# Scan coefficients and products in a PSUM bank per direction, input tables one block ahead, the last kernel block behind the first scan steps

## The chip, the cores and the metric

One core of one Trainium2 chip runs the whole forward pass of a small encoder trunk for one sequence of 512 positions and 1024 channels, in float32. The metric is the device time of one execution in microseconds. Five engines work side by side, each through its own queue in order: PE (matrix products), DVE and POOL (elementwise), ACT (elementwise with functions, and copies), SP (starts most DMA transfers). They wait for each other through semaphores. A line such as L669 is a line of the kernel before.

## What is computed

The trunk has two layers, each a mixer followed by a gated MLP. The first mixer is a bidirectional diagonal state-space model (S5), the second a differential attention. This change touches the S5 mixer and the gate behind it. Cut to that, the reference says:

```
def s5_mixer(h, lam_re, lam_im, log_step, b_re, b_im, c_re, c_im, d_skip, glu_w, glu_b):
    u = h.reshape(bsz, seq, S5_GROUPS, S5_GROUP)          # 64 groups of 16 channels
    y = (u * d_skip...)
    for direction in range(2):
        abar, bbar = ...                                  # from lam, log_step and B, 64 states a group
        bu = einsum('blgc,gpc->lbgp', u, bbar)            # complex
        s = associative_scan(s[l] = abar * s[l-1] + bu[l], reverse=(direction == 1))
        y = y + real(einsum('lbgp,gcp->blgc', s, c))
    g = gelu(y)
    return g * sigmoid(g @ glu_w + glu_b)
...
h = h + s5_mixer(rmsnorm(h)); h = h + conv_ffn(rmsnorm(h)); h = h + diff_attention(...); h = h + conv_ffn(...)
```

## The kernel before

The 512 positions are 64 blocks of 8. Inside a block the recurrence is a fixed 8 by 8 kernel, applied by matrix products (`intra`, tables `TT`); between blocks a scan of 64 steps carries the complex state of all groups, both directions side by side.

**Block stage** (L526 to L582). The loop over `b` takes 16 pairs of (8 groups, direction). For each, DVE multiplies the input matrices with a table of powers, `F` (L500, and L507 into PSUM), and adds the two (L537). PE transposes the result (`vtp`, L545), ACT copies it out (`vt`, L547), PE projects the input of the previous block into `ips` (L474), ACT copies that into `IZ` (L481), and PE builds kernel taps `kps` (L561). After every second block ACT copies the taps to `kq` (L571); two blocks later DVE repairs 16 columns of them (`kfix`, L514 and L516), PE transposes (`ktp`, L487) and ACT files them in `KF` and `KB` (L489). Four sets of 16 groups each have their `F`, with two buffers; `ftab` makes a set with 8 small ACT instructions (L385), and `tables` makes the powers `PR`, `PI` and the scan coefficients `sct` with 20 more (L451, L459). A counter at the end of each block (L573 to L578) says how many of each ACT takes there. `WOPS` says after which blocks POOL builds chunks of the output matrices `W` (L431, L433, L436; 16 chunks in all).

**Handover** (L584 to L617). After the last block come the repair and transposition of the last taps, then 15 DMAs that build `TT` out of `KF` and `KB`, then two ACT copies of the coefficients into the PSUM tile `scn`, then the scan.

**Scan** (L656 to L678). Each step has six DVE instructions: one product of state and coefficients for each direction (L669, 128 values a partition, out of PSUM into PSUM), one addition of the block's input for each direction (L672, 64 values), one addition into the next state (L674, 64 values). One tile `scn` of one PSUM bank holds the coefficients `cft` and products `prd` of both directions. Every 8 steps ACT files the states in `IZ` (`states`, L643, 8 copies) and the state goes into another buffer of the pool `syp`, which has 4.

**Behind the scan** PE, ACT and POOL do what is ready. The list `EV` sets where in the program each piece stands: at which step a chunk of `W` is built ('w'), an `intra` is run ('i'), a result is parked in SBUF ('y'), or half of the states' output is added ('f', 'b': `out_half`, L628). For the chunks in `PC` POOL makes the two products and PE adds them through an identity matrix (`wa`, L441 and L442), with ACT copying the sum back (L443). `NB` is the number of the 8 output blocks whose PSUM bank stays open until the end.

**Output and gate.** After the scan `out_fin` (L697) adds what is left, applies GELU, and `chan` (L728) transposes to channels. The gate (L847 to L865) runs 8 units `m`: 24 matrix products on PE, then ACT a tanh (L861), DVE two combinations (L863, L864), ACT the next layer's `xhi` and squares (L787, L791). A weight comes as float32 and is split into a high part by ACT (`hi`, L139) and a low part by DVE (`lo`, L141), one half unit at a time (`ws.split`). Then the MLP starts with `up(0)` (L933).

Of the kernel before, what the change touches and what calls it, by code (L numbers as in the profile page):

```python
# [37 lines left out]
def trunk(ctx, tc, xs, xt, sp, bx, cx, sv, vec, lamv, biasw, wglu, wup, wdn, wv, wqk, wo, out):  # L38
# [381 lines left out]
    def wbuild():  # L420
        for c in range(16):
            b4, hf, dr = c // 4, c // 2 % 2, c % 2
            if c % 4 == 0:
                W.append(arena(F32, [128, 2, 16, 8, 16], f"W{b4}"))
            d0 = dr * 64 + (2 * b4 + hf) * 8
            dst = W[b4][:, dr, hf * 8:hf * 8 + 8]
            w2 = (cpool if c % 2 or c < C0 else w2p).tile([128, 8, 8, 16], F32, tag="w2", name="w2", bufs=1)
            a1, a2 = PR[:, :, d0:d0 + 8], PI[:, :, d0:d0 + 8]
            if dr == 1:
                a1, a2 = a1[:, ::-1], a2[:, ::-1]  # L430
            G.tensor_tensor(w2, bc(X2, d0), kbc(a2), op=ALU.mult)  # L431
            yield
            G.tensor_tensor(dst, bc(X1, d0), kbc(a1), op=ALU.mult)  # L433
            yield
            if c not in PC:
                G.tensor_tensor(dst, dst, w2, op=ALU.add)  # L436
            else:
                for i in range(2):
                    wa = ps2.tile([128, 4, 8, 16], F32, tag="yp", name="wa", bufs=7)
# [24 lines left out]
    def in_mm(b, vts):  # L464
        p2, dr = divmod(b, 2)
        if b < 15:
            ips = ps1.tile([128, 4, 2, 64], F32, tag="ips", name="ips", bufs=1)
        else:
            ips = ps1.tile([128, 8, 2, 64], F32, tag="vb2", name="ips", bufs=1)[:, 0:4]
# [40 lines left out]
    def kfix(p2):  # L510

        kq, kp = kqs[p2], kpst.pop(p2)
        for q in range(2):
# [4 lines left out]
    WOPS = {5: 6, 6: 6, 9: 6}  # L518
    EV = ((7, 'w', 6), (11, 'i', 7), (11, 'y', 0), (12, 'i', 0), (13, 'i', 1), (14, 'i', 2), (15, 'i', 3), (18, 'w', 7), (19, 'w', 8), (29, 'w', 9),
# [3 lines left out]
    PC, C0 = (6, 8, 10, 12, 13, 14), 6  # L523
    kpst = {}
    vnext = vmul(0)
    for b in range(18):  # L526
# [27 lines left out]
        if b < 16:  # L554
# [26 lines left out]
        for _ in range(WOPS.get(b, 0)):  # L581
            next(wgen)  # L582

    vs.release()  # L584
    ps1.release()
    tp = pool("tp", 1, "left")
    TT = tp.tile([128, 8, 64, 16], F32, name="TT")
    for t in range(8):
        SY.dma_start(out=TT[0:16 * (t + 1), t], in_=KF[16 * (7 - t):128])
        if t < 7:  # L590
            SY.dma_start(out=TT[16 * (t + 1):128, t], in_=KB[16:16 * (8 - t)])
    ps2 = pool("ps2", 1, space=PSUM)
# [3 lines left out]
    w2p = pool("w2p", 1, "right")  # L596
# [3 lines left out]
    S.copy(cft[:, :, 0], sct[:, 0:64].rearrange("p (d r) -> p d r", d=2).unsqueeze(2).to_broadcast([128, 2, 2, 32]))  # L600
    S.copy(cft[:, :, 1], sct[:, 64:192].rearrange("p (d i r) -> p d i r", d=2, i=2)[:, :, ::-1])

    def intra(bk):
        yp = ps2.tile([128, 4, 8, 16], F32, tag="yp", name="yp", bufs=7)
# [7 lines left out]
    NB = 7  # L612
    ys = syp.tile([128, 4, 8, 16], F32, tag="yy", name="ys")
    for _ in range(3 * C0 - sum(WOPS.values())):
        next(wgen)
# [35 lines left out]
    for at_s, kind, bk in EV:  # L651
        f = {"w": wchunk, "i": lambda bk=bk: intra(bk), "y": lambda: S.copy(ys, yb.pop(NB)), "f": lambda bk=bk: out_half(bk, 0, 0),
# [3 lines left out]
    for s in range(64):  # L656
        sl = s % 8
        for f in plan.get(s, ()):
            f()
        cur = St[:, sl]  # L660
        if s < 63:
# [6 lines left out]
            for dr in range(2):  # L668
                V.tensor_tensor(prd[:, dr], cur[:, dr].unsqueeze(1).to_broadcast([128, 2, 2, 32]), cft[:, dr], op=ALU.mult)  # L669
            for dr in range(2):  # L670
                j = s if dr == 0 else 63 - s
                V.tensor_tensor(acc[dr], prd[:, dr, 0], IZ[:, j, dr], op=ALU.add)  # L672
            for dr in range(2):
                V.tensor_tensor(nx[:, dr], prd[:, dr, 1, ::-1], acc[dr], op=ALU.add)  # L674
# [22 lines left out]
    def out_fin(bk):  # L697
        if bk >= NB:
            yb[bk] = ps2.tile([128, 4, 8, 16], F32, tag="yp", name="yp", bufs=7)
# [22 lines left out]
        if bk >= NB:  # L722
            V.tensor_tensor(ys, y, ys, op=ALU.add)
            y = ys
# [3 lines left out]
    def chan(blk):  # L728
# [5 lines left out]
        for hf in range(2):  # L734
            tr = ps2.tile([128, 2, 64, 4], F32, tag="yp", name="tr", bufs=7)
# [111 lines left out]
    for un in range(4):  # L847
        wh, wl = ws.start()
        for ml in range(2):
            m = 2 * un + ml  # L850
            ws.split(ml, "h")
# [12 lines left out]
            V.scalar_tensor_tensor(h[:, m], th, 0.5, h[:, m], op0=ALU.mult, op1=ALU.add)  # L864
            norm_part(m, C_FFN0, m == 0)  # L865
# [610 lines left out]
```

## Time and profile before

| | us |
|---|---|
| median of 3 runs | 1285.21 (1283.9 to 1285.62) |
| profiled execution, its time | 1282.55 |
| its span on the core | 1280.7 |
| block stage, 22.9 to 98.1 | 75.2 |
| scan, 98.1 to 181.1 | 83.0 |
| output, 181.1 to 197.9 | 16.8 |
| gate, 197.9 to 246.7 | 48.8 |

PE is busy for 93% of the span, DVE for 66%, ACT for 45%, POOL for 20%. These are averages over stages with different limits: from 300 us on PE is busy almost without a break, and before 247 us it mostly waits for others. A stage is read by asking what ended each engine's idle time there.

### The profile page before, as it was taken

The numbers are of one execution on the slowest core, as the hardware profiler recorded it, in microseconds if no ns is written. First come the engines' busy times: TensorE is split into PE (matmuls) and PEld (weight loads), VectorE is DVE, ScalarE is ACT, GpSimd is POOL, SyncE is SP. The second block draws the span as 40 slices with busy tenths as digits, with TensorE's granted clock in tenths as the row PEclk, the third lists the DMA queues.
The fourth block names the chain that finished last, engine by engine and source line by source line (L and its number), as shares of the span: only waits on it lengthen the run. The fifth ranks groups of instructions, "written<-read, shape, count | busy, mean of one in ns | idle before, by whom it ended". The sixth has DMA issues, their size and how long they took to land.

```text
span 1280.7 us, 16573 instructions
## 1 busy us (share of the span) xinstructions
PE 1191.1 (93%) x6378; PEld 939.4 (73%) x6378; DVE 848.8 (66%) x1649; ACT 581.1 (45%) x1000; POOL 253.5 (20%) x270
## 2 busy tenths in 40 slices
PE   3884859899999999999999999999999999999996
PEld 1663438788887888878886777678888878888786
DVE  8878977767764256764437999886766753476633
ACT  6763444444442134443235778764544432344431
POOL 3957623400000000001003344432100000000011
PEclk8987879999999999999999999899999999999998
DMA  5005041322223312222232322301222233222221
GB/s 213 2 2 132 1 157 46 102 73 89 99 78 114 122 66 99 89 91 84 83 127 82 87 75 78 128 34 67 99 98 78 78 114 111 69 96 99 86 96 66
DMA packets 23391, 112.32 MB, mean 88 GB/s; under 512 B 2704, under 2 KB 5392, under 8 KB 16144
## 3 DMA queue, kind: packets, MB, share of 16 engines
q1 hardware_dynamic: 21472, 108.64, 25.0%
q0 software_dynamic: 1280, 2.10, 0.9%
q8 instruction: 50, 0.82, 0.3%
q10 hardware_dynamic: 560, 0.52, 0.1%
q14 instruction: 29, 0.24, 0.1%
HBM read 102.86 MB, written 2.10 MB: 82 GB/s over the span
## 4 chain that ended last, share of the span: by engine, by line
PE 79%; DVE 14%; ACT 4%; issue 2%; DMA 0%; SPq 0%; DVEq 0%; ACTq 0%
PE ps L770 18%; PE ps L769 18%; PE ps L771 18%; DVE scn L669 3%; DVE acc L672 2%; PE pj L769 2%; PE pj L771 2%; PE pj L770 2%; DVE St L674 1%; PE vtp L545 1%; PE po L770 1%; PE po L769 1%; PE po L771 1%; PE vps L1076 1%; DVE qkt L1129 1%
## 5 line engine op out<-in xcount | busy, mean ns | idle before, releaser
L769 PE MATMUL ps<-xhi,hi 128*128 128x512 f32 x672 | 267.0, 397 | 0.0
L770 PE MATMUL ps<-xlo,hi 128*128 128x512 f32 x672 | 265.8, 396 | 0.0
L771 PE MATMUL ps<-xhi,lo 128*128 128x512 f32 x672 | 264.3, 393 | 0.0
L139 ACT ACTIVATE hi<-raw 128x1024 fp32r<-128x1024 f32 (+2 forms) x216 | 184.0, 874 | 112.8 <-PE ps L770 85.9
L141 DVE TENSOR_TENSOR lo<-raw,hi 128x1024 fp32r<-128x1024 f32 (+3 forms) x178 | 191.1, 1093 | 55.3 <-ACT hi L139 53.6
L891 DVE TENSOR_TENSOR tpb<-ps,rb 128x512 f32<-128x512 f32 x88 | 60.8, 693 | 149.0 <-PE ps L771 143.4
L771 PEld LDWEIGHTS ps<-xhi,lo 128*128 128x128 f32 x672 | 126.2, 188 | 31.5
L769 PEld LDWEIGHTS ps<-xhi,hi 128*128 128x128 f32 x672 | 126.2, 188 | 30.6
L770 PEld LDWEIGHTS ps<-xlo,hi 128*128 128x128 f32 x672 | 126.2, 188 | 29.5
L893 ACT ACTIVATE acc<-tpb,vect 128x512 f32<-128x512 f32 x88 | 71.5, 815 | 167.7 <-DVE tpb L891 167.7
L770 PE MATMUL ps<-act,hi 128*128 128x512 f32 (+1 forms) x374 | 144.2, 386 | 0.2
L769 PE MATMUL ps<-act,hi 128*128 128x512 f32 (+1 forms) x374 | 142.9, 382 | 0.0
L771 PE MATMUL ps<-act,lo 128*128 128x512 f32 (+1 forms) x374 | 142.1, 380 | 0.0
L794 POOL COPY ssum<-sqt 128x512 f32<-128x512 f32 x4 | 2.5, 628 | 657.0 <-ACT sqt L791 657.0
L969 DVE TENSOR_TENSOR h<-ps,h 128x512 f32<-128x512 f32 x30 | 20.7, 691 | 107.4 <-PE ps L771 107.4
L141 POOL TENSOR_TENSOR lo<-raw,hi 128x512 fp32r<-128x512 f32 (+1 forms) x38 | 60.8, 1605 | 127.2 <-ACT hi L139 127.1
L771 PEld LDWEIGHTS ps<-act,lo 128*128 128x128 f32 x374 | 70.2, 188 | 15.9 <-DVE lo L141 1.4
L769 PEld LDWEIGHTS ps<-act,hi 128*128 128x128 f32 x374 | 70.3, 188 | 15.7
L770 PEld LDWEIGHTS ps<-act,hi 128*128 128x128 f32 x374 | 70.3, 188 | 15.3 <-DVE act L910 1.1
L899 DVE SCALAR_TENSOR_TENSOR acc<-tpb,vect,acc 128x512 f32<-128x512 f32 x88 | 66.2, 752 | 3.1
L898 DVE SCALAR_TENSOR_TENSOR acc<-tpb,vect,acc 128x512 f32<-128x512 f32 x88 | 65.5, 745 | 0.6 <-ACT acc L893 0.6
L909 ACT ACTIVATE act<-acc 128x512 fp32r<-128x512 f32 x44 | 27.9, 633 | 66.9 <-DVE acc L908 66.9
(260 smaller groups left out, 2072.4 us busy)
## 6 DMA issues: line engine op xcount, KB each, us to landing
raw<-wup SPq DMA_DIRECT2D x44, 1024.0 KB, 4.8
raw<-wdn SPq DMA_DIRECT2D x32, 704.0 KB, 4.0
raw<-wqk SPq DMA_DIRECT2D x16, 512.0 KB, 3.5
raw<-wglu SPq DMA_DIRECT2D x4, 1024.0 KB, 4.8
raw<-wv SPq DMA_DIRECT2D x8, 512.0 KB, 3.4
raw<-wo SPq DMA_DIRECT2D x4, 1024.0 KB, 4.8
bias<-biasw SPq DMA_DIRECT2D x8, 448.0 KB, 4.1
cxt<-cx SPq DMA_DIRECT2D x1, 2064.0 KB, 15.9
```

The costliest lines, as they stand in the source:

```text
L139: S.activation(hi[:, h0:h1], self.raw[i][:, h0:h1], AF.Copy)
L141: eng.tensor_tensor(lo[:, h0:h1], self.raw[i][:, h0:h1], hi[:, h0:h1].bitcast(F32), op=ALU.subtract)
L669: V.tensor_tensor(prd[:, dr], cur[:, dr].unsqueeze(1).to_broadcast([128, 2, 2, 32]), cft[:, dr], op=ALU.mult)
L672: V.tensor_tensor(acc[dr], prd[:, dr, 0], IZ[:, j, dr], op=ALU.add)
L769: PE.matmul(ps, lhsT=wh, rhs=xh, start=first, stop=False)
L770: PE.matmul(ps, lhsT=wh, rhs=xl, start=False, stop=False)
L771: PE.matmul(ps, lhsT=wl, rhs=xh, start=False, stop=last)
L891: V.tensor_tensor(tb[:, 1:513], ps, state["rb"], op=ALU.mult)
L893: S.activation(acc, tb[:, 1:513], AF.Identity, bias=cb, scale=cw[1])
L898: V.scalar_tensor_tensor(acc, tb[:, 0:512], cw[0], acc, op0=ALU.mult, op1=ALU.add)
L899: V.scalar_tensor_tensor(acc, tb[:, 2:514], cw[2], acc, op0=ALU.mult, op1=ALU.add)
L909: S.activation(hi, a0, AF.Copy)
```

## The change

1. The tile `scn` becomes two, `scn0` and `scn1`, one PSUM bank for each direction, and `cft` and `prd` become lists. The second bank is the one that `ips` had, now in the pool `psc`; the last two `ips` (blocks 14 and 15) share one tile with the tag of `vb2`. The pool of the scan's other PSUM tiles shrinks from 7 banks to 6.
2. `ftab` for the third and fourth sets starts after blocks 3 and 7, not 4 and 8, with 4 instructions a block; `tables` goes by a list of counts that leaves those blocks alone and ends three blocks later.
3. The repair, transposition and filing of the last taps (`kfix(7)`, `kt(7)`) and the 15 DMAs move into `toeplitz()`, called at scan step 2.
4. POOL builds 8 chunks of `W` in the block stage, not 6. `EV` puts the rest at other steps; the chunks that PE adds are 8, 10, 12, 13 and 14 (6 was one before). `NB` is 6: two output blocks are parked in `ys` and finished after the scan, not one.
5. In the gate the high split of the next half unit stands behind this unit's tanh and its two combinations, ahead of `norm_part`; before, it stood at the head of the next unit.

The diff, without renamed bufs and indices:

```diff
     def in_mm(b, vts):
-        if b < 15:
-            ips = ps1.tile([128, 4, 2, 64], F32, tag="ips", name="ips", bufs=1)
+        if b < 14:
+            ips = psc.tile([128, 4, 2, 64], F32, tag="t", name="ips", bufs=1)
         else:
-            ips = ps1.tile([128, 8, 2, 64], F32, tag="vb2", name="ips", bufs=1)[:, 0:4]
+            if b == 14:
+                vtt["i"] = ps1.tile([128, 8, 2, 64], F32, tag="vb2", name="ips", bufs=1)
+            ips = vtt["i"][:, 4 * (b - 14):4 * (b - 13)]
...
-    WOPS = {5: 6, 6: 6, 9: 6}
+    WOPS = {5: 6, 6: 6, 9: 12}
...
-    PC, C0 = (6, 8, 10, 12, 13, 14), 6
+    PC, C0 = (8, 10, 12, 13, 14), 8
-    for b in range(18):
+    for b in range(16):
...
-            if b in (4, 8):
-                fgen = ftab(2 + b // 8)
-            for _ in range(3):
+            if b in (3, 7):
+                fgen = ftab(2 + b // 7)
+            for _ in range(4):
                 next(fgen, None)
-            for _ in range(2 if b > 0 else 0):
+            for _ in range((0, 3, 3, 0, 0, 2, 2, 0, 0, 2, 2, 2, 2, 2)[b] if b < 14 else 0):
                 next(tgen, None)
...
+    def toeplitz():
+        kfix(7)
+        kt(7, kqs.pop(7))
+        vs.release()
+        ps1.release()
+        tp = pool("tp", 1, "left")
+        TT = tp.tile([128, 8, 64, 16], F32, name="TT")
+        for t in range(8):
+            SY.dma_start(out=TT[0:16 * (t + 1), t], in_=KF[16 * (7 - t):128])
...
-    scn = psc.tile([128, 2, 2, 2, 2, 32], F32, tag="s", name="scn", bufs=1)
-    cft, prd = scn[:, 0], scn[:, 1]
+    cft, prd = [], []
+    for dr in range(2):
+        scn = psc.tile([128, 4, 2, 2, 32], F32, tag="st"[dr], name=f"scn{dr}", bufs=1)
+        cft.append(scn[:, 0])
+        prd.append(scn[:, 1])
...
-    NB = 7
+    NB = 6
...
     for s in range(64):
+        if s == 2:
+            tp, TT, ps2, w2p = toeplitz()
...
-                V.tensor_tensor(prd[:, dr], cur[:, dr].unsqueeze(1).to_broadcast([128, 2, 2, 32]), cft[:, dr], op=ALU.mult)
+                V.tensor_tensor(prd[dr], cur[:, dr].unsqueeze(1).to_broadcast([128, 2, 2, 32]), cft[dr], op=ALU.mult)
...
     for un in range(4):
         wh, wl = ws.start()
+        if un == 0:
+            ws.split(0, "h")
         for ml in range(2):
             m = 2 * un + ml
-            ws.split(ml, "h")
...
             V.scalar_tensor_tensor(h[:, m], th, 0.5, h[:, m], op0=ALU.mult, op1=ALU.add)
+            if m < 7:
+                ws.split(1 - ml, "h")
             norm_part(m, C_FFN0, m == 0)
```

The table `EV` and the buffers set the order of the instructions; at three places it reads as follows.

DVE in the scan before, one step with its waits on earlier instructions of its own queue (`scn` holds both directions' coefficients and products, `acc` and `St` the sums and the state):

```order
L669 TENSOR_TENSOR scn<-St,scn 128x128 [waits DVE_49] x2
L672 TENSOR_TENSOR acc_1232<-scn,IZ 128x64 [waits DVE_49]
L672 TENSOR_TENSOR acc_1233<-scn,IZ 128x64
L674 TENSOR_TENSOR St<-scn,acc_1232 128x64 [waits DVE_49]
L674 TENSOR_TENSOR St<-scn,acc_1233 128x64 [waits DVE_49]
```

And DVE of the change, the second step and the repair that now stands behind it:

```order
L678 TENSOR_TENSOR scn_1204<-St,scn_1204 128x128 [waits DVE_49]
L678 TENSOR_TENSOR scn_1207<-St,scn_1207 128x128 [waits DVE_49]
L681 TENSOR_TENSOR acc_1202<-scn_1204,IZ 128x64 [waits DVE_49]
L681 TENSOR_TENSOR acc_1203<-scn_1207,IZ 128x64 [waits DVE_49]
L683 TENSOR_TENSOR St<-scn_1204,acc_1202 128x64 [waits DVE_49]
L683 TENSOR_TENSOR St<-scn_1207,acc_1203 128x64 [waits DVE_49]
L516 SCALAR_TENSOR_TENSOR kq<-svt,kps 128x16 [waits PE_49]
```

The instructions and their order in a step are the same. In the program before, both products and the first addition wait for the instruction directly ahead of them; in the changed one each of the six waits for the instruction two places ahead, which is of its own direction.

PE in the second half of the scan before (`yp` is an output bank, `wa` a chunk's sum, `W` the output matrices, `ident` the identity):

```order
L628 MATMUL yp<-W_617,IZ 32x128 x32
L628 MATMUL yp<-W_857,IZ 32x128 x32
L441 MATMUL wa<-W_1697,ident 128x512
L442 MATMUL wa<-w_1698,ident 128x512
L441 MATMUL wa<-W_1697,ident 128x512
L442 MATMUL wa<-w_1698,ident 128x512
L628 MATMUL yp<-W_1434,IZ 32x128 x16
```

And PE of the change there:

```order
L633 MATMUL yp<-W_617,IZ 32x128 x32
L441 MATMUL wa<-W_1622,ident 128x512
L442 MATMUL wa<-w_1623,ident 128x512
L441 MATMUL wa<-W_1622,ident 128x512
L442 MATMUL wa<-w_1623,ident 128x512
L633 MATMUL yp<-W_853,IZ 32x128 x32
L441 MATMUL wa<-W_1622,ident 128x512
```

A chunk's addition now stands between the first and the second pair of output blocks, and two more chunks follow directly behind the second.

ACT in the gate before (`hi` the high part of a weight, `th` the tanh, `xhi` and `sqt` what the next layer's norm needs):

```order
L139 ACTIVATE hi_2476<-raw_2394 128x1024
L861 ACTIVATE th<-ps,hb 128x512
L787 ACTIVATE xhi<-h,vect 128x512
L791 ACTIVATE sqt<-h 128x512
L139 ACTIVATE hi_2476<-raw_2394 128x1024
```

And ACT of the change there:

```order
L871 ACTIVATE th<-ps,hb 128x512
L139 ACTIVATE hi_2451<-raw_2379 128x1024
L796 ACTIVATE xhi<-h,vect 128x512
L800 ACTIVATE sqt<-h 128x512
L871 ACTIVATE th<-ps,hb 128x512
```

The high split of the next half unit stands between a unit's tanh and its `xhi`, so it no longer waits behind `xhi` and `sqt`.

## Rows read from the trace of the kernel before

**Rows 1.** Busy time in the scan: us; busy of PE, PEld, DVE, ACT, POOL; clock, DMA.

```profile
98.10:181.10 83.00, 48.10 (x400) 28.89 (x400) 76.56 (x379) 31.75 (x72) 48.27 (x24) 0.81 0.34 102
```

**Rows 2.** Timeline of DVE, block stage: start us, us, engine, line, operation [idle before].

```profile
54.85 1.22 DVE L500 TENSOR_TENSOR vb<-bxt,F 128x1024 f32<-128x1024 f32 x1 [3.08 <-ACT F L385]
...
62.44 0.37 DVE L514 SCALAR_TENSOR_TENSOR kq<-svt,kps 128x16 f32<-128x16 f32 x2 [0.46 <-ACT kq L571]
...
62.95 1.21 DVE L500 TENSOR_TENSOR vb<-bxt,F 128x1024 f32<-128x1024 f32 x1
...
73.32 1.22 DVE L500 TENSOR_TENSOR vb<-bxt,F 128x1024 f32<-128x1024 f32 x1 [2.75 <-ACT F L385]
...
81.61 0.37 DVE L514 SCALAR_TENSOR_TENSOR kq<-svt,kps 128x16 f32<-128x16 f32 x2 [1.16 <-ACT kq L571]
```

**Rows 3.** Busy time in one short stretch of the block stage, columns as rows 1.

```profile
57.50:60.80 3.30, 3.30 (x39) 2.85 (x39) 3.27 (x4) 1.07 (x2) 3.22 (x2) 0.50 0.00 0
```

**Rows 4.** Timeline of ACT and DVE at the handover, columns as rows 2.

```profile
93.47 0.58 ACT L481 COPY IZ<-ips 128x512 f32<-128x512 f32 x1 [0.93 <-PE ips L474]
94.40 0.58 ACT L481 COPY IZ<-ips 128x512 f32<-128x512 f32 x1 [0.35 <-PE ips L474]
...
95.72 0.27 ACT L489 COPY KB<-ktp 128x128 f32<-128x128 f32 x1
...
97.48 0.27 ACT L600 COPY scn<-sct 128x128 f32<-128x128 f32 x1
...
98.09 0.63 DVE L669 TENSOR_TENSOR scn<-St,scn 128x128 f32<-128x128 f32 x2 [1.73 <-ACT scn L601]
```

**Rows 5.** Timeline of DVE, one scan step and the next one's products.

```profile
98.75 0.36 DVE L672 TENSOR_TENSOR acc<-scn,IZ 128x64 f32<-128x64 f32 x2
99.02 0.34 DVE L674 TENSOR_TENSOR St<-scn,acc 128x64 f32<-128x64 f32 x2
99.40 0.63 DVE L669 TENSOR_TENSOR scn<-St,scn 128x128 f32<-128x128 f32 x2
```

**Rows 6.** The tile scn over the scan: count, ns min/median/max, first and last start.

```profile
L669 DVE TENSOR_TENSOR scn<-St,scn x126: 295/295/298, 98.1 to 180.1; 128x128 f32<-128x128 f32 x126
L672 DVE TENSOR_TENSOR acc<-scn,IZ x126: 214/220/227, 98.8 to 180.5; 128x64 f32<-128x64 f32 x126
L674 DVE TENSOR_TENSOR St<-scn,acc x126: 214/214/225, 99.0 to 180.8; 128x64 f32<-128x64 f32 x126
```

**Rows 7.** Timeline of DVE, a product into PSUM with an instruction that doesn't wait behind.

```profile
24.18 1.23 DVE L507 TENSOR_TENSOR vb<-bxt,F 128x1024 f32<-128x1024 f32 x1
25.31 1.22 DVE L500 TENSOR_TENSOR vb<-bxt,F 128x1024 f32<-128x1024 f32 x1
```

**Rows 8.** Timeline of PE in the scan.

```profile
129.88 2.08 PE L441 MATMUL wa<-W,ident 128*128 128x512 f32 x2 [4.13 <-POOL W L433]
...
136.54 1.09 PE L609 MATMUL yp<-TT,u 128*64 128x128 f32 x16
...
148.49 1.13 PE L441 MATMUL wa<-W,ident 128*128 128x512 f32 x2
...
152.12 1.61 PE L628 MATMUL yp<-W,IZ 128*32 128x128 f32 x32
```

**Rows 9.** Timeline of ACT in the scan, one filing of states.

```profile
150.27 3.33 ACT L643 COPY IZ<-St 64x256 f32<-64x256 f32 x8 [7.22 <-DVE acc L672]
```

**Rows 10.** Timeline of POOL, first products of two neighbouring chunks.

```profile
48.39 2.03 POOL L431 TENSOR_TENSOR w<-cxt,PI 128x1024 f32<-128x1024 f32 x1 [1.44 <-ACT PI L451]
...
54.93 2.02 POOL L431 TENSOR_TENSOR w<-cxt,PI 128x1024 f32<-128x1024 f32 x1
```

**Rows 11.** Timeline of PE in the output: seventh and eighth block.

```profile
192.44 1.12 PE L716 MATMUL yp<-W,IZ 128*32 128x128 f32 x32
193.50 2.09 PE L704 MATMUL yp<-W,IZ 128*64 128x128 f32 x32
```

**Rows 12.** Timeline of PE at the end of the gate.

```profile
246.72 0.50 PE L933 MATMUL ps<-xhi,hi 128*128 128x512 f32 x1 [3.27 <-ACT hi L139]
```

More of the change, by code (lines that the diff above doesn't have):

```diff
@@ L438, in wbuild @@
                 for i in range(2):
-                    wa = ps2.tile([128, 4, 8, 16], F32, tag="yp", name="wa", bufs=7)
+                    wa = ps2.tile([128, 4, 8, 16], F32, tag="yp", name="wa", bufs=6)
                     part = slice(4 * i, 4 * i + 4)
@@ L582, in trunk @@
             next(wgen)
[L584 to L592, printed above, removed]
+    def toeplitz():
[7 more added lines that the diff above has]
+            SY.dma_start(out=TT[0:16 * (t + 1), t], in_=KF[16 * (7 - t):128])
+            if t < 7:
+                SY.dma_start(out=TT[16 * (t + 1):128, t], in_=KB[16:16 * (8 - t)])
+        return tp, TT, pool("ps2", 1, space=PSUM), pool("w2p", 1, "right")
     yb = {}
-    w2p = pool("w2p", 1, "right")
     acc = [s5c.tile([128, 2, 32], F32, name=f"acc{i}") for i in range(2)]
-    scn = psc.tile([128, 2, 2, 2, 2, 32], F32, tag="s", name="scn", bufs=1)
-    cft, prd = scn[:, 0], scn[:, 1]
-    S.copy(cft[:, :, 0], sct[:, 0:64].rearrange("p (d r) -> p d r", d=2).unsqueeze(2).to_broadcast([128, 2, 2, 32]))
-    S.copy(cft[:, :, 1], sct[:, 64:192].rearrange("p (d i r) -> p d i r", d=2, i=2)[:, :, ::-1])
+    cft, prd = [], []
[3 more added lines that the diff above has]
+        prd.append(scn[:, 1])
+        S.copy(cft[dr][:, 0], sct[:, 32 * dr:32 * dr + 32].unsqueeze(1).to_broadcast([128, 2, 32]))
+        S.copy(cft[dr][:, 1], sct[:, 64 + 64 * dr:128 + 64 * dr].rearrange("p (i r) -> p i r", i=2)[:, ::-1])
     def intra(bk):
-        yp = ps2.tile([128, 4, 8, 16], F32, tag="yp", name="yp", bufs=7)
+        yp = ps2.tile([128, 4, 8, 16], F32, tag="yp", name="yp", bufs=6)
         yb[bk] = yp
@@ L610, in intra @@
                           skip_group_check=True)
-    NB = 7
-    ys = syp.tile([128, 4, 8, 16], F32, tag="yy", name="ys")
-    for _ in range(3 * C0 - sum(WOPS.values())):
-        next(wgen)
+    NB = 6
     St = syp.tile([128, 8, 2, 2, 32], F32, tag="yy", name="St")
@@ L651, in trunk @@
     for at_s, kind, bk in EV:
-        f = {"w": wchunk, "i": lambda bk=bk: intra(bk), "y": lambda: S.copy(ys, yb.pop(NB)), "f": lambda bk=bk: out_half(bk, 0, 0),
+        f = {"w": wchunk, "i": lambda bk=bk: intra(bk), "y": lambda bk=bk: S.copy(ys[:, bk - NB], yb.pop(bk)), "f": lambda bk=bk: out_half(bk, 0, 0),
              "b": lambda bk=bk: out_half(bk, 1, 1)}[kind]
@@ L657, in trunk @@
         sl = s % 8
+        if s == 2:
+            tp, TT, ps2, w2p = toeplitz()
+        if s == 16:
+            ys = syp.tile([128, 2, 4, 8, 16], F32, tag="yy", name="ys")
         for f in plan.get(s, ()):
@@ L698, in out_fin @@
         if bk >= NB:
-            yb[bk] = ps2.tile([128, 4, 8, 16], F32, tag="yp", name="yp", bufs=7)
+            yb[bk] = ps2.tile([128, 4, 8, 16], F32, tag="yp", name="yp", bufs=6)
             for pl in range(4):
@@ L722, in out_fin @@
         if bk >= NB:
-            V.tensor_tensor(ys, y, ys, op=ALU.add)
-            y = ys
+            V.tensor_tensor(ys[:, bk - NB], y, ys[:, bk - NB], op=ALU.add)
+            y = ys[:, bk - NB]
         S.activation(Yt[bk // 2][:, :, (bk % 2) * 4:(bk % 2) * 4 + 4], y.rearrange("p r t c -> p t r c"),
@@ L734, in chan @@
         for hf in range(2):
-            tr = ps2.tile([128, 2, 64, 4], F32, tag="yp", name="tr", bufs=7)
+            tr = ps2.tile([128, 2, 64, 4], F32, tag="yp", name="tr", bufs=6)
             for t in range(4):
```

6 lines of the change are left out of this document (3 added, 3 removed), and 6 rows, old and new, of the table EV.

## Prediction

> **What bounds the kernel now.** I read the busy time by stage first. In the scan DVE is busy for 76.56 of 83.00 us and no other engine for more than 49 [rows 1], so the scan is as long as its DVE instructions. The timeline then shows a step: 1.31 us from the first products to the next ones [rows 4, 5], 63 times. The sizes show that this is not all work. A product takes 0.295 us and two take 0.63, so the second starts 0.03 us after the first has ended; an addition takes 0.22, yet two take 0.36, so the second starts 0.14 after the first, while that still runs [rows 5, 6]. An instruction that waits for its predecessor pays about 0.12 us that one without such a wait doesn't pay. Three instructions a step pay it: both products and the first addition.
>
> Ahead of the scan DVE is the engine others feed and wait for; its idle times there are four: 3.08 and 2.75 us for `F`, which ACT writes, 0.46 and 1.16 us for `kq`, which ACT copies [rows 2]. The first two are ACT being late with a table, the other two their echo: right behind the first, PE's granted clock is 0.50, its 1.2 GHz level [rows 3], after PE had stood without new blocks, and the taps come late. Behind the scan, the gate's PE stands still for 3.27 us at its end, waiting for a high split [rows 12]. From there on PE is the bound to the end of the program, so what is won before that is kept.
>
> **The change part by part.** *Tables a block ahead.* The third and fourth `F` are done a block before DVE asks for them. That removes 3.08 + 2.75 us. PE keeps getting blocks, so the slow clock behind each stall and with it 0.46 + 1.16 us should go too: 7.45 us. ACT has the same instructions in all, and the new counts put three tables into blocks 1 and 2; if ACT is late there instead, up to the 1.62 us of the echo come back. I take 7.45, range 5.8 to 7.45.
>
> *Handover.* Now the repair of the last taps, their transposition and two filings stand between the next-to-last filing and the coefficient copies; that filing ends at 95.72 + 0.27 = 95.99, the first product starts at 98.09 [rows 4]. After the change the copies follow at once. From the start of the first copy to the product it is 98.09 - 97.48 = 0.61, so 1.49 us go. But blocks 14 and 15 now share one `ips` tile, so the projection of 15 waits until ACT has copied 14. The copy of 14 ends at 93.47 + 0.58 = 94.05; the pitch of the two projections is 94.40 - 93.47 = 0.93; so the second copy starts at about 95.0 to 95.2, not 94.40: 0.7 us, with `kps`, `kq` and the filing queued behind it. The repair moves into DVE's queue behind step 1 and costs 62.95 - 62.44 = 0.51 us [rows 2]; its input is ready by then. Its DMAs go past nothing on SP. Net gain 0.3.
>
> *The scan.* Every wait is now for the instruction two places ahead. What starts without a wait: behind an addition 0.14 or (0.36 - 0.22, 0.34 - 0.21) 0.13 us after its start [rows 5]; behind a product the nearest row is a PSUM write of 1.23 us whose successor starts 25.31 - 24.18 = 1.13 us later, 0.09 before its end [rows 7], which for a product gives 0.295 - 0.09 = 0.205. A step is 2 x 0.205 + 0.14 + 3 x 0.13 = 0.94; I take 0.95. Are the waits then met? The tightest is the first state addition: it starts 0.27 after the first addition did, which takes 0.22 plus the 0.03 seen between a wait's end and a start. It holds by 0.02. So 1.31 - 0.95 = 0.36 us for 62 step distances: 22.5 us. Bounds: if the products cannot overlap with what follows, since no row shows two of them without a wait, 0.25 a step is lost, step 1.2, and the gain is 7; below 0.94 nothing.
>
> On this a page of the Trainium skill speaks against the change. "VectorE: DVE Perf Modes", section "The DRAIN you can't avoid", says that the next DVE instruction does not start until the pipeline has emptied and that semaphores between instructions cost nothing; by that the step would stay at 1.31. The pairs of rows 5 disagree: two additions take 0.36, not 0.44. The page itself lets an instruction that nothing holds start earlier in its next section.
>
> *What runs behind the scan.* The steps from 32 on now take 32 x 0.95 = 30.4 us, and PE has in them six pairs of halves of 1.61, three chunk additions of 152.12 - 148.49 = 3.63 and two `intra` of 1.09 [rows 8]: 22.8. It fits, but one chain is tight. ACT files the states of step 39 only behind the copies of chunks 12 and 13, and the scan's write at the end of step 55 reuses a buffer and waits for that filing. From the filing of step 31 on the chain is four halves 3.2, an addition 3.6, four halves 3.2, an addition 3.6, a copy 0.6, a filing 3.3 [rows 8, 9]: 17.5. It has 24 steps or 22.8 us less the first filing's 3.3, so 19.5 and a slack of 2. That filing itself may be late: POOL now makes 8 chunks at a pitch of 54.93 - 48.39 = 6.54 [rows 10] before the scan's own, the second one from about 52 as its table comes a block later, which ends at about 98, eight us into the scan; chunk 10 is out of POOL at about 112, its addition on a slow clock takes 136.54 - 129.88 = 6.66 [rows 8], and `intra` 7, its parking copy and the filings of steps 23 and 31 queue behind. That makes the filing of 31 some 3 us late. I take a stall of 1.5 us, range 0 to 4.
>
> *Output.* The seventh block now takes a full pass: 2.09 for 1.12 us [rows 11], and a DVE addition that lies beside the eighth. PE and with it the gate start 1.0 later. A parked `y6` costs nothing, since it lies beside the scan.
>
> *Gate.* The high split no longer queues behind `xhi` and `sqt`. ACT and DVE then run ahead of PE, whose 3.27 us of idle time go [rows 12]; what is late next is nothing before the first MLP unit's own products. Range 2.5 to 3.27.
>
> Sum: 7.45 + 0.3 + 22.5 - 1.5 - 1.0 + 3.3 = 31.0 us. The profiled execution took 1282.55 (span 1280.7 and 1.85 around it), which becomes 1251.5; the median of the runs, 1285.21, becomes **1254.2**. The chain's bounds make 1250 to 1259 of it.
>
> **The rivals.** *The tail takes over.* If the clock stays at its lower level while PE works behind the scan, the three additions cost 6.66 each and not 3.63, two of them in the chain above: 6 us more, and up to 9 if all PE work ends behind the scan. For it: PE's mean clock in the scan is 0.81 [rows 1], and PE waits before each batch. Against it: the work is denser now, and the batch at 148.49 ran at 3.63. It gives 1259 to 1264.
>
> *No overlap behind a product.* The step is 1.2 (only the additions gain), or stays at 1.31 if the two banks change nothing. For it: no row has a product without a wait behind it that is a PSUM write again. Against it: rows 7. With the longer step the stall of 1.5 goes: 1254.2 + 15.5 - 1.5 = 1268, or 1275 with no gain at all. That last is also what the page's rule gives, and the case in which the change does not do what it says.
>
> *The tables stay late.* ACT is in order, and a set of 4 `F` stands behind the same copies as before. If DVE still waits, 7.45 us are missing: 1262. Against it: the lead is a whole block, about 4 us, and the longest wait was 3.08.
>
> *Slower than before: six instructions in file.* Now each instruction works in another bank than its predecessor. If a change of bank made DVE finish the predecessor first, all six would wait as three do now: 2 x 0.33 + 2 x 0.25 + 2 x 0.25 = 1.66 a step, 0.35 x 62 = 22 us lost and not 22.5 won, and no stall: 1254.2 + 44.3 - 1.5 = 1297. The other parts win about 10, so this decides from a step of 1.31 + 10 / 62 = 1.47 on. Against it: rows 7 go from PSUM to SBUF without any pause.
>
> **How the numbers follow.** Forecast 0.62 (1250 to 1259), tail 0.16, no overlap 0.13 (half of it at 1268, half at 1275), late tables 0.05, slower 0.04 with all other ways to lose. The range of 1249 to 1266 holds the forecast, the tail and the late tables, 0.83 less what falls outside at its ends. A measurement of this kernel tells about 0.2%, 2.6 us, from no change. All cases but the last are faster by more: faster 0.95, same 0.01, slower 0.04.
>
> **What would show it.** Right: no DVE idle time before L500 in the block stage; two products in about 0.5 us, not 0.63, and a step of 0.95 in the scan's timeline; DVE idle for ACT at the end of step 55 alone; no idle PE time at the start of `up(0)`; the gate 45 us long. Wrong: a step over 1.0; the scan's end set by ACT or PE; a first product later than 91 us; new idle times of PE in the gate.

## The result and the profile after

The changed kernel takes 1248.57 us (median of 4 runs, 1246.88 to 1249.9); before took 1284.56 beside it. The ratio is 0.9719, with a 95% interval of 0.9701 to 0.9737. That is 36 us, where 31 were forecast, and 0.4 us under the range's lower end. In a later session the same program took 1249.1. Medians are of executions at one speed: one of the kernel with the tables back took 1293.9 at a granted clock of 0.929, where its other three had 0.975 to 0.977, and is in no median here.

The profiled execution took 1246.88 (span 1245.1). The first view is the busy time by stage: us; busy of PE, PEld, DVE, ACT, POOL; clock, DMA. The stages are block stage, scan, output and gate; the second row answers to [rows 1].

```profile
22.90:90.50 67.60, 53.22 (x924) 41.01 (x924) 60.16 (x72) 47.77 (x117) 60.84 (x49) 0.92 0.01 2
90.50:149.90 59.40, 39.30 (x364) 24.41 (x364) 59.12 (x382) 30.90 (x72) 46.79 (x23) 0.86 0.38 107
149.90:168.10 18.20, 15.54 (x289) 14.29 (x289) 7.58 (x19) 11.20 (x23) 5.64 (x3) 0.91 0.45 175
168.10:213.00 44.90, 44.90 (x195) 35.99 (x193) 29.48 (x47) 23.42 (x34) 19.14 (x15) 1.00 0.23 76
```

DVE is now busy for 59.12 of the scan's 59.40 us, and PE for every moment of the gate. The second view is DVE's timeline in one scan step and the next one's products, as [rows 5]:

```profile
93.95 0.48 DVE L678 TENSOR_TENSOR scn<-St,scn 128x128 f32<-128x128 f32 x2
94.34 0.35 DVE L681 TENSOR_TENSOR acc<-scn,IZ 128x64 f32<-128x64 f32 x2
94.61 0.34 DVE L683 TENSOR_TENSOR St<-scn,acc 128x64 f32<-128x64 f32 x2
94.87 0.48 DVE L678 TENSOR_TENSOR scn<-St,scn 128x128 f32<-128x128 f32 x2
```

A step is 94.87 - 93.95 = 0.92 us, where it was 1.31. Two products take 0.48 and not 0.63, and the additions follow 0.39 after the first product's start (94.34 - 93.95). The third view is the tile `scn` over the scan, as [rows 6] (ns min/median/max):

```profile
L678 DVE TENSOR_TENSOR scn<-St,scn x126: 283/288/295, 90.5 to 149.0; 128x128 f32<-128x128 f32 x126
L681 DVE TENSOR_TENSOR acc<-scn,IZ x126: 214/215/229, 91.1 to 149.4; 128x64 f32<-128x64 f32 x126
```

An instruction takes nearly as long as it did (288 for 295 ns, 215 for 220); what shrank is the distance from one start to the next.

Of DVE's idle times in the block stage [rows 2], those for `F` are gone. Two small ones for `kq` stand there that the first profile of before does not have, and ahead of the scan DVE waits for the coefficients:

```profile
36.44 0.37 DVE L516 SCALAR_TENSOR_TENSOR kq<-svt,kps 128x16 f32<-128x16 f32 x2 [0.23 <-ACT kq L573]
...
44.48 0.37 DVE L516 SCALAR_TENSOR_TENSOR kq<-svt,kps 128x16 f32<-128x16 f32 x2 [0.41 <-ACT kq L573]
...
90.48 0.69 DVE L678 TENSOR_TENSOR scn<-St,scn 128x128 f32<-128x128 f32 x2 [4.29 <-ACT scn L609]
```

Only the second of the two, 0.41, is new. The first is there in the second profile of before too (0.36), and in the kernel with the tables back (0.72). The last, 4.29, takes the place of two in before: 1.73 [rows 4] and, for the last `kq` at 95.62, 2.59.

The table sets the stages of two executions of each kernel side by side (the second ones, below under "The same programs once more"). The stages run from the first table product on DVE to the first scan product, the last state addition, the first and the last gate product, the last product of the attention's output, and the end.

| us | forecast | before | after | before, again | after, again |
|---|---|---|---|---|---|
| start to first table product | 0 | 22.9 | 23.2 | 24.0 | 24.8 |
| block stage and handover | -8.3 | 75.15 | 67.29 | 75.33 | 67.63 |
| scan | -20.5 | 82.92 | 59.37 | 82.68 | 59.55 |
| output | +1.0 | 16.88 | 18.22 | 17.18 | 16.55 |
| gate, first to last product | 0 | 44.70 | 44.70 | 44.69 | 44.70 |
| on to the end of the attention | -3.3 | 651.94 | 646.11 | 653.30 | 647.90 |
| rest | 0 | 386.2 | 386.2 | 386.2 | 386.2 |
| span | -31 | 1280.7 | 1245.1 | 1283.4 | 1247.3 |

The forecast's terms are put into these stages; the repair (0.51) and the stall (1.5) count to the scan. Two rows hold what was missed: the scan won about 3 us more (3.1 and 2.6 in the two pairs), and the stretch behind the gate about 2 us more (2.5 and 2.1).

### The profile page after: what moved, and what is told of

Same layout as the page of the kernel before. It is cut to its first block, busy times and chain, and to the rows that moved or that the text cites. A ratio compares the mean times of both kernels' runs of the same rounds, so it can differ in the third digit from the quotient of the medians.

```text
span 1245.1 us, 16497 instructions
## 1 busy us (share of the span) xinstructions
PE 1175.8 (94%) x6338; PEld 930.0 (75%) x6338; DVE 824.9 (66%) x1650; ACT 581.6 (47%) x1001; POOL 253.5 (20%) x271
## 4 chain that ended last, share of the span: by engine, by line
PE 83%; DVE 14%; ACT 2%; issue 1%; DMA 0%; SPq 0%; DVEq 0%; ACTq 0%
PE ps L779 20%; PE ps L778 20%; PE ps L780 20%; DVE scn L678 2%; PE pj L778 2%; PE pj L780 2%; PE pj L779 2%; DVE St L683 1%; PE vps L1088 1%; DVE qkt L1141 1%; PE vps L1090 1%; PE vps L1089 1%; DVE acc L681 1%; PE po L779 1%; PE po L780 1%; PE po L778 1%
## 5 line engine op out<-in xcount | busy, mean ns | idle before, releaser
L141 DVE TENSOR_TENSOR lo<-raw,hi 128x1024 fp32r<-128x1024 f32 (+3 forms) x178 | 188.3, 1077 | 43.5 <-ACT hi L139 41.8
L780 PEld LDWEIGHTS ps<-act,lo 128*128 128x128 f32 x374 | 70.2, 188 | 15.9 <-DVE lo L141 1.4
```

Source lines behind the costliest of these rows:

```text
L141: eng.tensor_tensor(lo[:, h0:h1], self.raw[i][:, h0:h1], hi[:, h0:h1].bitcast(F32), op=ALU.subtract)
L780: PE.matmul(ps, lhsT=wl, rhs=xh, start=False, stop=last)
```

## The experiments

Four kernels undo one edit each, one reorders the scan step, three go further, and two repeat the programs. Each is the changed kernel with the edit shown, cut to its main lines. No run undoes the fourth edit (chunks of `W`, `EV`, `NB`) or the shared `ips` tile by itself.

**One tile for both directions.**

```diff
+    scn = psc.tile([128, 2, 2, 2, 2, 32], F32, tag="s", name="scn", bufs=1)
     for dr in range(2):
-        scn = psc.tile([128, 4, 2, 2, 32], F32, tag="st"[dr], name=f"scn{dr}", bufs=1)
-        cft.append(scn[:, 0])
-        prd.append(scn[:, 1])
+        cft.append(scn[:, 0, dr])
+        prd.append(scn[:, 1, dr])
```

> The changed kernel with one edit undone: coefficients and products of both directions lie in one tile of one PSUM bank again; tables, taps, output matrices and gate stay as changed. Theory (the scan gained because three instructions of a step no longer wait for the one directly ahead): the step goes from 0.92 back to 1.31 us, 63 x 0.39 = 24.6 us, the median from 1248.6 to about 1273. Rival (the scan gained because other work was moved out of its way): the step stays below 1.0 and the median below 1255.

Measured: 1272.05 us, ratio to before 0.990 (0.9885 to 0.9914). The step is back, in DVE's timeline:

```profile
93.32 0.35 DVE L683 TENSOR_TENSOR St<-scn,acc 128x64 f32<-128x64 f32 x2
93.70 0.63 DVE L678 TENSOR_TENSOR scn<-St,scn 128x128 f32<-128x128 f32 x2
94.36 0.36 DVE L681 TENSOR_TENSOR acc<-scn,IZ 128x64 f32<-128x64 f32 x2
94.63 0.35 DVE L683 TENSOR_TENSOR St<-scn,acc 128x64 f32<-128x64 f32 x2
```

94.63 - 93.32 = 1.31. The scan takes 83.3 us; the split alone is worth 23.0 to 23.5 of the 36 us. The split gives each direction a tile and a bank of its own; two tiles in one bank were not run, so which of the two takes the waits away is not shown.

**One direction after the other.** Both tiles stay; the loops over the directions become one, so that each addition follows what it waits for.

```diff
             for dr in range(2):
                 V.tensor_tensor(prd[dr], ..., op=ALU.mult)
-            for dr in range(2):
                 j = s if dr == 0 else 63 - s
                 V.tensor_tensor(acc[dr], prd[dr][:, 0], IZ[:, j, dr], op=ALU.add)
-            for dr in range(2):
                 V.tensor_tensor(nx[:, dr], prd[dr][:, 1, ::-1], acc[dr], op=ALU.add)
```

> The changed kernel with the six instructions of a scan step in another order: product, input addition and state addition of one direction, then the same three of the other. Both banks, all instructions and all their sizes stay; the additions now wait for the instruction directly ahead of them (four waits a step), the products for none. Theory (a wait for the direct predecessor costs 0.12 to 0.14 us, whatever the bank): a step of 2 x (0.33 + 0.25 + 0.13) = 1.42 us, 63 x 0.50 = 31.5 us more, about 1280. Rival (two banks let VectorE run at 0.92 and waits between its own instructions cost nothing): the step stays at 0.92.

Measured: 1278.04 us in one execution, a step of 1.44. DVE's timeline of half a step (one direction) and the next product:

```profile
100.23 0.29 DVE L678 TENSOR_TENSOR scn<-St,scn 128x128 f32<-128x128 f32 x1
100.55 0.22 DVE L680 TENSOR_TENSOR acc<-scn,IZ 128x64 f32<-128x64 f32 x1
100.81 0.22 DVE L681 TENSOR_TENSOR St<-scn,acc 128x64 f32<-128x64 f32 x1
100.95 0.29 DVE L678 TENSOR_TENSOR scn<-St,scn 128x128 f32<-128x128 f32 x1
```

And the tiles over the scan (ns min/median/max):

```profile
L678 DVE TENSOR_TENSOR scn<-St,scn x126: 285/286/295, 90.3 to 181.2; 128x128 f32<-128x128 f32 x126
L680 DVE TENSOR_TENSOR acc<-scn,IZ x126: 224/224/225, 90.7 to 181.5; 128x64 f32<-128x64 f32 x126
```

The gaps tell it: 0.32 behind a product of 0.29 and 0.26 behind an addition of 0.22, so 0.03 to 0.04 after the end, where the next one waits; 0.14 behind an addition where the next does not, 0.08 before the end. The same instructions on the same two banks, in an order with four such waits a step, give up the whole gain of the scan, which takes 91.7 us (82.9 in before). So it is not the banks that make DVE faster, it is the distance between an instruction and the one it waits for; the split takes away the waits that no data asked for.

**The tables where they were.**

```diff
-            if b in (3, 7):
-                fgen = ftab(2 + b // 7)
-            for _ in range(4):
+            if b in (4, 8):
+                fgen = ftab(2 + b // 8)
+            for _ in range(3):
                 next(fgen, None)
-            for _ in range((0, 3, 3, 0, 0, 2, 2, 0, 0, 2, 2, 2, 2, 2)[b] if b < 14 else 0):
+            for _ in range(2 if b > 0 else 0):
                 next(tgen, None)
```

> The changed kernel with one edit undone: the third and fourth input tables are issued after blocks 4 and 8, three instructions a block, and the powers two a block, as before. Theory (the tables' place made VectorE wait): idle times of about 3.1 and 2.8 us for F return, with a low clock and an idle time for kq behind each, and the first product of the scan comes 5.8 to 7.5 us later; the median is 1254.4 to 1256. Rival (PE or POOL would have hidden it anyway): under 2 us later.

Measured: 1254.3 us (median of 3), ratio 0.9763 (0.9747 to 0.9779). The idle times of [rows 2] for `F` return on DVE, and behind each a shorter one for `kq` (0.45 and 0.26):

```profile
56.95 1.22 DVE L502 TENSOR_TENSOR vb<-bxt,F 128x1024 f32<-128x1024 f32 x1 [3.10 <-ACT F L385]
...
75.43 1.22 DVE L502 TENSOR_TENSOR vb<-bxt,F 128x1024 f32<-128x1024 f32 x1 [2.76 <-ACT F L385]
```

From the first table product to the scan it takes 98.66 - 24.44 = 74.2 us against 67.3 and 67.6: the edit is worth 6.6 to 6.9 there. Between the medians it is 5.2 to 5.7.

**The gate's high split where it was.**

```diff
-        if un == 0:
-            ws.split(0, "h")
         for ml in range(2):
             m = 2 * un + ml
+            ws.split(ml, "h")
...
-            if m < 7:
-                ws.split(1 - ml, "h")
             norm_part(m, C_FFN0, m == 0)
```

> The changed kernel with one edit undone: in the gate the high split stands at the head of its own unit again. Theory (it queued behind xhi and sqt): PE stands idle for about 3.3 us ahead of up(0), the gate takes 48.2 to 48.8 us instead of 44.9, the median is 1252. Rival (the gate gained from the second layer of the weights arriving earlier, or from the shifted start): no idle time, within 1 us of 1248.6.

Measured: 1253.39 us, ratio 0.9754 (0.9739 to 0.9769), so 4.3 to 4.8 more than the changed kernel and not 3.3. The idle time is back on PE, in its timeline:

```profile
217.04 0.79 PE L942 MATMUL ps<-xhi,hi 128*128 128x512 f32 x1 [3.35 <-ACT hi L139]
```

And behind it PE's granted clock, last but two in the busy time of the stretch, is 0.50, the 1.2 GHz level:

```profile
217.40:219.60 2.20, 2.20 (x6) 1.72 (x6) 2.17 (x3) 0.16 (x1) 0.05 (x1) 0.50 0.13 15
```

The first product there takes 0.79 us; the one at the same place in [rows 12] took 0.50. The gap can bring a slow stretch with it that the first profile of before did not happen to show.

**The last taps ahead of the scan.** `toeplitz()` is called ahead of the coefficient copies and not at step 2.

```diff
+    tp, TT, ps2, w2p = toeplitz()
     yb = {}
...
-        if s == 2:
-            tp, TT, ps2, w2p = toeplitz()
```

> The changed kernel with one edit undone: repair, transposition and filing of the last taps and the 15 DMAs stand ahead of the coefficient copies again, not behind scan step 1. Theory: the first product comes about 2.0 us later, the repair's 0.5 us leave the scan, net 1.5 us, median 1250.1. Rival (the last input projection decides when the scan starts): the first product comes less than 0.5 us later and the median does not move up.

Measured: 1247.86 us, ratio 0.971 (0.9693 to 0.9726): no difference to the changed kernel that the runs can tell. The mechanism is there: the scan starts 93.60 - 24.53 = 69.1 us behind the first table product, 1.4 to 1.8 later, and takes 58.7, 0.6 to 0.8 less. The net of 0.6 to 1.1 lies inside what two executions differ by. So the median did not rise by 1.5 as expected, although the first product came later as expected.

**The same programs once more.**

> The changed kernel once more, for what differs between two executions of the same program. Theory: the stages up to the gate agree within 1 us from the first table product on, and the stretch from the gate to the end of the attention differs by up to 4 us, where PE's granted clock falls in one execution and not in the other; median 1248.6 within 1. Rival: that stretch takes 646 us again and the difference lies ahead of the scan.

> The kernel before once more, for what differs between two executions. Theory: from the first table product to the first gate product it takes 174.9 us within 0.5 again; the stretch from the gate's last product to the last product of the attention takes 649.4 (without the 2 us in which PE's granted clock falls) or 651.9 us as in the first profile, by chance. Rival: the 2 us belong to the kernel before and come every time.

Measured: 1249.1 and 1285.16 us. From the first table product to the first gate product before takes 175.2 (174.95 the first time) and after 143.7 (144.9), 1.2 apart where 1 was expected, by the output stage. The stretch to the end of the attention is 653.3 and 651.9 in before, 646.1 and 647.9 in after; 653.3 is above both values that were expected. The views below show why. The first two are the busy time in 5 us of the attention, at the same place in the program, in after again and in after:

```profile
667.90:672.90 5.00, 5.00 (x19) 3.69 (x16) 4.07 (x11) 3.79 (x8) 0.57 (x1) 0.66 0.58 174
```

```profile
667.50:672.50 5.00, 5.00 (x25) 3.72 (x24) 4.93 (x14) 3.83 (x8) 0.54 (x1) 1.00 0.58 193
```

The third and fourth are PE's timeline at the gate's idle time in before again, and the busy time in the 4.4 us behind it:

```profile
248.07 0.79 PE L933 MATMUL ps<-xhi,hi 128*128 128x512 f32 x1 [3.33 <-ACT hi L139]
```

```profile
248.20:252.60 4.40, 4.40 (x11) 3.43 (x12) 4.07 (x5) 2.06 (x4) 0.57 (x2) 0.50 0.46 134
```

PE is busy throughout in each stretch, and the same 5 us of the attention hold 19 of its instructions or 25. Over all profiles: of the nine without the gate's idle time, five take 646.1 to 646.5 us here and four 647.8 to 648.3, with such falls; none has one right behind the gate. Of the three with the idle time, two have one there, and all three have one later.

What the idle time costs is read from DVE's first instruction of the MLP, in the timelines of after, before, before again and the kernel with the gate's split back:

```profile
231.07 1.29 DVE L903 TENSOR_TENSOR tpb<-ps,rb 128x512 f32<-128x512 f32 x2 [2.61 <-ACT rb L827]
...
264.42 1.29 DVE L891 TENSOR_TENSOR tpb<-ps,rb 128x512 f32<-128x512 f32 x2 [2.60 <-ACT rb L818]
...
268.29 1.29 DVE L891 TENSOR_TENSOR tpb<-ps,rb 128x512 f32<-128x512 f32 x2 [2.60 <-ACT rb L818]
...
236.23 1.29 DVE L900 TENSOR_TENSOR tpb<-ps,rb 128x512 f32<-128x512 f32 x2 [2.61 <-ACT rb L827]
```

The last gate products start at 212.77, 242.59, 243.88 and 212.83, so it comes 18.3, 21.8, 24.4 and 23.4 us behind them. The 3.3 us of idle time cost 3.5 us in one execution without a fall of the clock there, and 6.1 and 5.1 in the two with one. About 2 us of the attention are chance.

**Coefficients early.** Ahead of the scan DVE still stands for 4.29 us. Here the coefficient tiles and their copies move ahead of the last two projections, and the projection of block 15 gets a bank of its own.

```diff
-            if b == 14:
-                vtt["i"] = ps1.tile([128, 8, 2, 64], F32, tag="vb2", name="ips", bufs=1)
-            ips = vtt["i"][:, 4 * (b - 14):4 * (b - 13)]
+            ips = ps1.tile([128, 4, 2, 64], F32, tag="F", name="ips", bufs=2) if b == 15 else ps1.tile([128, 8, 2, 64], F32, tag="vb2", name="ips", bufs=1)[:, 0:4]
...
         if b == 15:
+            for dr in range(2):
+                scn = psc.tile([128, 4, 2, 2, 32], F32, tag="st"[dr], name=f"scn{dr}", bufs=1)
+                ...
             in_mm(14, vtt.pop(14))
             in_mm(15, vtt.pop(15))
```

> The changed kernel with two more edits ahead of the scan: the four coefficient copies are issued ahead of the projections of blocks 14 and 15, and the projection of block 15 has a PSUM bank of its own, so it no longer waits for the copy of block 14. The first addition then starts behind the copy of block 15, about 2.8 us earlier against the end of the block stage. Theory (the chain of output matrices, halves and state filings behind the scan is within 0.2 us of binding): VectorE stands idle at the end of step 55 for about 3 us, the scan ends no earlier, median 1248.6 within 0.7. Rival (that chain has slack): no idle time there and a median of about 1245.8.

Measured: 1248.92 us, no change. The additions start at 87.15 and 88.08, not at 91.07, but the scan ends at 149.89, not at 149.85. DVE's timeline at the end of step 55, then ACT's:

```profile
139.47 0.35 DVE L679 TENSOR_TENSOR acc<-scn,IZ 128x64 f32<-128x64 f32 x2
143.08 0.36 DVE L681 TENSOR_TENSOR St<-scn,acc 128x64 f32<-128x64 f32 x2 [3.26 <-ACT IZ L646]
```

```profile
139.74 3.31 ACT L646 COPY IZ<-St 64x256 f32<-64x256 f32 x8
```

The write into the reused state buffer waits for the filing of step 39, which ends at 139.74 + 3.31 = 143.05, and it ends there whether the scan comes early or not. The chain that the forecast described is real, and in the changed kernel it has no slack.

**And the order behind the scan.** Beside that, chunk 10 moves two steps later and `intra` 7 with its parking copy one step, behind the filing of the states of step 23, and the pool of the states gets a fifth buffer (the second pair of lines is a cut out of `EV`).

```diff
-    syp = pool("syp", 4, "left")
+    syp = pool("syp", 5, "left")
...
-(22, 'w', 10), (23, 'i', 7), (23, 'y', 7)
+(24, 'w', 10), (24, 'i', 7), (24, 'y', 7)
```

> The same, and chunk 10 of the output matrices is added behind the filing of the states of step 23, not ahead of it, and the states have a fifth buffer. Theory: the filings of steps 23 and 31 come 3 us earlier, PE goes on with the halves right behind the intra products, no idle time in the scan, the scan ends 2.8 us earlier than in the changed kernel, median about 1245.8. Rival (ACT's copies or POOL's chunks bind at the scan's end instead): the gain is under 1 us.

Measured: 1245.43 us, ratio 0.9702 (0.9689 to 0.9715), 3.1 to 3.7 less than the changed kernel. The scan ends 123.4 us behind the first table product (126.7 and 127.2 in the changed kernel), without an idle time of DVE in it. On ACT the filing of step 23 follows that of step 15 directly, and that of step 31 starts 97.6 us behind the first table product (100.5 in the changed kernel); on PE the halves follow `intra` at once. The two edits were not run apart. The filing of step 39 ends at 140.56, 117.0 us behind the first table product (119.8 in the run above): that is the order at work. The state addition at the end of step 55 starts at 140.21, before that filing ends, so it no longer writes into the buffer that is being filed: that is the fifth buffer. What either gives alone is not shown. ACT's timeline, then PE's:

```profile
109.06 6.63 ACT L646 COPY IZ<-St 64x256 f32<-64x256 f32 x16
...
121.25 3.35 ACT L646 COPY IZ<-St 64x256 f32<-64x256 f32 x8
```

```profile
118.64 5.46 PE L615 MATMUL yp<-TT,u 128*64 128x128 f32 x96
124.03 2.75 PE L631 MATMUL yp<-W,IZ 128*32 128x128 f32 x64
```

**POOL files a part.** One edit more, `G.tensor_copy` for the four backward copies of the states of steps 40 to 47.

```diff
-(V.tensor_copy if b8 == 56 and dr == 1 else S.copy)(dst, src)
+(V.tensor_copy if b8 == 56 and dr == 1 else G.tensor_copy if b8 == 40 and dr == 1 else S.copy)(dst, src)
```

> The kernel with early coefficients, the later chunk 10 and the fifth state buffer, and one edit more: POOL, idle then, files the four backward copies of the states of steps 40 to 47, not ACT. Theory (ACT's queue of 20 copies, 8.4 us without a gap around the scan's end, holds up the output by about 1.2 us against the program before): the first output product comes 1.2 to 1.6 us earlier against the scan's end, median about 1244. Rival (the last filing itself decides, whatever stands ahead of it): no change, 1245.4.

Measured: 1244.33 us (1242.47 to 1245.3), ratio 0.9683 (0.967 to 0.9697), the lowest median here, though 1.1 us below the kernel above is within what their runs spread. The first output product on PE, in the kernel above (scan end 147.01) and in this one (147.91):

```profile
149.26 0.43 PE L723 MATMUL yp<-W,IZ 128*32 128x128 f32 x2 [2.83 <-ACT IZ L646]
150.10 5.40 PE L723 MATMUL yp<-W,IZ 128*32 128x128 f32 x126 [0.41 <-ACT IZ L646]
```

```profile
148.69 0.43 PE L723 MATMUL yp<-W,IZ 128*32 128x128 f32 x2 [1.27 <-ACT IZ L646]
149.53 3.91 PE L723 MATMUL yp<-W,IZ 128*32 128x128 f32 x126 [0.41 <-ACT IZ L646]
```

It comes 0.8 us behind the scan's end and not 2.25, so 1.5 earlier. The second lines, 5.40 against 3.91 for the same 126 products, are the clock again: over the stage it is 0.91 in the first and 1.00 in the second. How much of that follows from the shorter wait stays open, since after again also had 1.00 there, with the long queue.

## Why the forecast was too high, step by step

What failed are sizes, not the mechanism: the scan's step, put at 0.95 us and measured at 0.92; the stall at step 55, put at 1.5 and measured at 0.2; and the clock behind the gate's idle time, put at nothing, so that 3.3 us stood for what cost 3.5 to 6.1. That the median lies 0.4 us outside the range is less than the two sessions of the program differ by, so the terms tell more than the total.

**What bounds** was read rightly: the scan is DVE's, DVE waited for `F` ahead of it, PE for a high split behind it, and all of it was kept to the end.

**Tables**, 7.45 in a range of 5.8 to 7.45: 6.6 to 6.9 by the undo. The wait of 0.41 for `kq` stands in all nine profiles with the new counts and in none with the old, so it is a part that comes back, as the forecast allowed for; whether the three tables in block 2 make it is not shown. **Handover**, 0.3 net: from DVE's last copy of `vt` to the first scan product it takes 98.09 - 92.34 = 5.75 us in before, 90.48 - 85.36 = 5.12 in after, and 93.60 - 87.02 = 6.58 with the taps back. So moving the taps gives 1.46 (forecast 1.49), and the rest, with the shared tile, takes 0.83 back (forecast 0.7): the projection of 15 waits, and ACT's copies stand 1.87 apart (86.49 and 88.36), not 0.93. The repair makes one step of the scan 0.50 longer (forecast 0.51), which leaves 0.1 net. Together these two terms gave 0.4 to 0.6 us less than the 8.3.

**The scan step** was mis-sized by 0.03 us, 62 times 0.03 or 1.8 us. The mechanism is as forecast, and two experiments carry it. Of the 0.03, 0.02 lie in the products: 0.39 for two, not 0.41, mostly because a product that overlaps is itself shorter, 0.288 and not the 0.295 taken from the waiting ones; 0.01 was rounding the sum of 0.94 up to 0.95. (The gain was also summed a little high: 0.36 times 62 is 22.3, not 22.5.) The rule of the Trainium skill ("VectorE: DVE Perf Modes", "The DRAIN you can't avoid") that a semaphore between instructions costs nothing, by which the step would have stayed at 1.31, does not hold here: the order with the waits gives 1.44, the one without 0.92. What the same section grants, that an instruction which nothing holds starts earlier, the 0.92 agrees with.

**The stall at step 55**: 1.5 forecast, 0.2 measured (0.3 in after again). The place and the wait are right, as DVE's timeline and then ACT's show:

```profile
142.59 0.35 DVE L681 TENSOR_TENSOR acc<-scn,IZ 128x64 f32<-128x64 f32 x2
143.04 0.36 DVE L683 TENSOR_TENSOR St<-scn,acc 128x64 f32<-128x64 f32 x2
```

```profile
139.70 3.31 ACT L648 COPY IZ<-St 64x256 f32<-64x256 f32 x8
```

The state addition starts 0.45 behind the input addition, and 0.27 in other steps (0.32 to 0.33 where the state goes into another buffer). The filing of step 31 ran late as forecast: it starts at 123.72, where step 31's first product starts at 119.88 and the filing of step 7, which nothing held up, started 0.64 behind that step's. By that it could have started at 120.5, so it is 3.2 late. A slack of 2 against 3 would have given a stall of 1.0 by the forecast's own figures, and the chain behind it was too long in the sum. Each four halves were put at 3.2, twice the 1.61 of one pair. PE's rows show them at less:

```profile
127.13 2.11 PE L633 MATMUL yp<-W,IZ 128*32 128x128 f32 x46 [0.41 <-ACT IZ L648]
129.17 1.12 PE L441 MATMUL wa<-W,ident 128*128 128x512 f32 x2
...
132.80 2.63 PE L633 MATMUL yp<-W,IZ 128*32 128x128 f32 x64
135.36 1.13 PE L441 MATMUL wa<-W,ident 128*128 128x512 f32 x2
```

135.36 - 132.80 = 2.56 for four halves: the pairs are pipelined, and a duration added twice counts the end of the first twice. The other four had begun while the filing still ran, and only 2.0 of them stand behind it. So the chain took 15.9 us (127.07 to 143.01) and not 17.5. An addition of a chunk took 132.80 - 129.17 = 3.63, as forecast.

**Output**, +1.0: +1.3 in one execution and -0.6 in the other. Over all profiles with the new scan the stage took 15.9 to 16.6 us where PE's mean clock in it was 1.00 and 17.0 to 18.6 where it was 0.90 or 0.91; in before it was 0.82 and 0.80. The full pass of the seventh block is in it, but this term was below what the clock makes of the stage.

**Gate**, 3.3: the idle time is gone, PE runs 213.00 and 213.24 without a gap, and the rows behind show nothing late.

```profile
212.77 0.39 PE L780 MATMUL ps<-gx,lo 128*128 128x512 f32 x1
213.00 0.40 PE L945 MATMUL ps<-xhi,hi 128*128 128x512 f32 x1
213.24 0.39 PE L946 MATMUL ps<-xlo,hi 128*128 128x512 f32 x1
```

The term is mis-sized all the same. The forecast charged the slow clock to the stalls in the block stage, and did not ask for it behind the gate's idle time, because the one profile of before showed none there (its late fall, some 2 us, lay far off in the attention). Undone, the edit costs 4.3 to 4.8 us in the median. In the first pair of profiles the gate's own part came out at 3.5, near the forecast, by luck, since before happened to have no fall there; the 2 us more in that row are before's late fall.

In sum: the scan's step 1.8 and the stall 1.3 too dear, the clock behind the gate and in the attention about 2, against 0.5 less ahead of the scan. That is 4.6 of the 5 to 5.6 us by which the medians lie under the forecast; the rest is within what executions differ by. The range's lower end stood 5.2 us under the forecast: the step and the stall took 3.1 of it, the first against a bound of "below 0.94 nothing" that took the products at the length of waiting ones, and for the clock behind the gate it held nothing.

**The rivals.** The tail did not take over: PE's clock was 1.00 from 118 us to the scan's end, and the chain bound by the 0.2 us alone. No overlap, late tables and six instructions in file did not come; the nearest to the last that was run is the order with four waits, 1278.

## What to carry to other kernels

On an engine whose instructions are as short as here, ask of each what it waits for and how far back that stands: 0.26 us from addition to addition against 0.13 was the difference between waiting for the direct predecessor and not, and a buffer shared by independent work made such waits where the data had none. When the bound stage is shortened, look at once for the chain beside it, and test its slack by starting the stage earlier: here the next 3 us were worth nothing until a filing of states moved ahead of a copy and the states had one more buffer. Sum a chain by distances between starts, not by durations, and charge an idle PE with the slow stretch that may follow it, even where the one profile at hand does not show it.

## What the runs showed of the hardware that was not expected

An instruction of DVE that has waited for its direct predecessor is also itself longer: the input addition takes 224 ns in the order by direction, where it waits so, and 215 in the changed kernel; the product, which waits for its direct predecessor in neither, takes 286 and 288, and 295 in before, where it does. And PE's granted clock falls to 0.50 behind an idle time of 3.3 us in two executions of three, not in the third, and inside the attention in some executions of a program and not in others, with PE busy in both; what decides it there, the runs don't tell.
